# Loading the second pieces of six early groups through ScalarE's DMA queue instead of SyncE's

## Chip, cores, metric

One core of a Trainium2 chip. The metric is the device time of one execution in microseconds (us), as the median of several executions; smaller is better. A profile shows a span about 2 us shorter than the time (96.6 us against 98.38 us for the profiled execution of the kernel before).

Words used below: **PE** is TensorE, **PEld** its weight loads, **DVE** VectorE, **ACT** ScalarE, **SPq** and **ACTq** the sequencers of SyncE and ScalarE, which issue transfers. A transfer "has landed" when the last of its 16 DMA engines has raised its completion semaphore.

## The reference

```python
rows, cols = 1024, 8192                       # x: float32
mean = np.mean(x, axis=-1, keepdims=True)
std = np.std(x, axis=-1, keepdims=True)
z = (x - mean) / (std + 1e-8)
return (np.mean(z ** 4, axis=-1) - 3).astype(np.float32)
```

The kurtosis of each row: 33.5 MB are read once and 4 KB written.

## The kernel before

The rows are cut into 18 groups, each laid over all 128 partitions. Groups 0 and 1 have 0.5 MB, group 2 has 1 MB, and groups 3 to 17 have 2 MB each, loaded in two to four pieces. I call the two pieces of group 3 "3a" and "3b", and so on.

```python
GROUPS = [                      # parts of a row, columns of each piece, columns of the 4th power on ACT
    (8, [1024], 0),             # group 0
    (8, [1024], 0),             # group 1
    (4, [2048], 0),             # group 2
    (2, [2048, 2048], 512),     # group 3: pieces 3a, 3b of 1 MB each
    # ... groups 4 to 12 are the same; 13 to 17 have three or four smaller pieces
]
SLOTS = 12                      # tiles of 2 MB for the data

def load(i):
    # ...
    c = 0
    for w in pieces:
        nc.sync.dma_start(out=xt[:, c:c + w], in_=src[:, c:c + w])
        c += w

def row_sums(i):                # groups 3 to 17: sums by 32 transposes on TensorE, first piece first
    # ...
    for c in range(0, w, P):
        nc.tensor.matmul(tps, lhsT=xt[:, c:c + P], rhs=ident,
                         start=c == 0, stop=c == w - P, is_transpose=True)
    nc.vector.tensor_reduce(out=red..., in_=tps..., op=AO.add, axis=AX)

def mean(i):
    nc.tensor.matmul(mps, lhsT=lhs, rhs=rhs, start=True, stop=True)
    nc.scalar.copy(nmu, mps)                       # "the copy": minus the mean

def square(i):
    nc.scalar.activation(out=xts[i], in_=xts[i], func=AF.Square, bias=nmus[i],
                         accum_out=sa[:, j:j + 1])

# fourth_act(i): 512 columns of the 4th power on ScalarE; fourth_dve(i): the rest on VectorE
# finish(b): for a batch of groups, two small matmul parts ("the reciprocal part" is the first),
#            a few small VectorE operations and a store

for i in range(NG):
    load(i)                     # every load stands ahead of all computing
waiting = []
for i in range(NG):
    row_sums(i)
    mean(i)
    square(i)
    # ... next step of a finish, fourth_dve(i - 1), fourth_act(i)
```

Each engine works through its own instructions in the order of the source. On TensorE, the mean of group 2 (it needs VectorE's sum of group 2) and the reciprocal part of the first batch (it needs the squares of groups 0 and 1) stand ahead of group 3's transposes.

## Time and profile before

| what | value | from |
|---|---|---|
| time, median of 2 | 98.88 us (98.24 to 99.53) | the runs |
| span | 96.6 us | the profile |
| busy: ACT, DVE, PE, PEld | 81, 75, 70, 64% | the page's part 1 |
| DMA engines full | slices 2 to 34 of 40, about 420 GB/s | the page's part 2 |
| last load landed | 84.58 us | semaphore events of the trace |
| square of group 3 begins | 18.86 us | timeline of ScalarE |
| square of group 17 begins | 86.80 us | timeline of ScalarE |

The slices give a first answer ("the DMA engines are full"), but they are an average over a start, a long middle and a tail. The timelines by engine tell what each stage waits for. A line of a timeline gives start, duration, engine, source line, operation, tiles; the bracket at its end is the idle time of the engine ahead of it and what ended that. The lines themselves are in the prediction below.

### The profile page before, as it was taken

Reading aid. Unit: us, or ns where it says so; the run is one execution under the profiler, and the core shown is the slowest. Engines: PE = TensorE matmul, PEld = TensorE weight load, DVE = VectorE, ACT = ScalarE, POOL = GpSimd, SP = SyncE. Lnnn points to the kernel's source line nnn. Section 1 sums busy time; section 2 is a strip of 40 time slices with the busy share of each in tenths; the row PEclk is TensorE's granted clock in tenths of the full one; section 3 lists DMA queues with packets and bytes.
Section 4 is the critical chain, followed back from the end, with each engine's and each line's share of the span. In section 5 each row is a group of like instructions: output and inputs, shape, how many; then the busy total and the mean of one; then the engine's idle time right before and its main releaser. Section 6 shows DMA issues by size and latency. Waiting matters only on the chain.

```text
span 96.6 us, 1451 instructions
## 1 busy us (share of the span) xinstructions
PE 67.5 (70%) x540; PEld 61.4 (64%) x540; DVE 72.2 (75%) x74; ACT 77.9 (81%) x86; POOL 4.7 (5%) x20
## 2 busy tenths in 40 slices
PE   0040699797959597979797979797978797950120
PEld 0040699696949496969686868696967696940010
DVE  0238600653969998989898989798989698999470
ACT  6055540299979889999999999899999899989960
POOL 6830000000000000000000000000000000000000
PEclk9999999999999999999999999999999999998555
DMA  1999999999999999999999999999999999200000
GB/s 47 398 395 410 420 427 427 434 431 424 414 410 424 434 417 417 417 431 427 400 431 417 431 404 420 395 427 407 423 409 421 407 419 395 113 1 0 0 0 0
DMA packets 5658, 33.64 MB, mean 348 GB/s; under 512 B 660, under 2 KB 660, under 8 KB 2964
## 3 DMA queue, kind: packets, MB, share of 16 engines
q1 hardware_dynamic: 5652, 33.56, 84.5%
q8 instruction: 4, 0.07, 0.3%
q14 instruction: 2, 0.02, 0.0%
HBM read 33.55 MB, written 0.00 MB: 347 GB/s over the span
## 4 chain that ended last, share of the span: by engine, by line
DMA 72%; PE 13%; ACT 7%; SPq 3%; DVE 2%; issue 1%; ACTq 0%
DMA xt<-in_x_dram 72%; PE tps L132 10%; ACT xt L158 4%; SPq L120 3%; ACT xt L165 3%; DVE red L135 1%; PE mps L151 1%; PE p L191 1%; PE p L192 0%; DVE kr L194 0%; PE p L182 0%; DVE kr L195 0%; ACTq L252 0%; ACTq L158 0%; ACT nmu L153 0%
## 5 line engine op out<-in xcount | busy, mean ns | idle before, releaser
L171 DVE CUSTOM_DVE_ANT_0 xt<-xt 128x3584 f32<-128x3584 f32 (+3 forms) x18 | 60.6, 3365 | 1.9 <-ACT nmu L153 1.1
L158 ACT ACTIVATE xt<-xt,nmu 128x4096 f32<-128x4096 f32 (+2 forms) x18 | 60.1, 3342 | 0.8
L132 PE MATMUL tps<-ident,xt 128*128 128x128 f32 x480 | 59.6, 283 | 1.0 <-DMA xt<-in_x_dram 1.0
L132 PEld LDWEIGHTS tps<-ident,xt 128*128 128x128 f32 x480 | 55.5, 148 | 3.1 <-DMA xt<-in_x_dram 2.6
L135 DVE TENSOR_REDUCE red<-tps 128x128 f32<-128x256 f32 x15 | 6.3, 423 | 11.7 <-PE tps L132 11.4
L153 ACT COPY nmu<-mps 128x1 f32<-128x1 f32 x18 | 2.7, 151 | 13.2 <-PE mps L151 13.2
L151 PEld LDWEIGHTS mps<-negcol,red 128*128 128x128 f32 x30 | 4.5, 188 | 13.1 <-ACT xt L158 6.5
L151 PE MATMUL mps<-negcol,red 128*128 128x1 f32 x30 | 5.4, 248 | 9.9 <-DVE red L135 7.0
L165 ACT ACTIVATE xt<-xt 128x512 f32<-128x512 f32 (+1 forms) x15 | 11.4, 759 | 0.5
L151 PE MATMUL mps<-part,blk 128*128 128x1 f32 x6 | 1.7, 353 | 9.0 <-DVE part L143 9.0
L151 PEld LDWEIGHTS mps<-part,blk 128*128 128x128 f32 x6 | 1.5, 312 | 9.2 <-POOL blk L78 5.2
L143 DVE CUSTOM_DVE_ANT_0 junk<-xt 128x512 bf16<-128x512 f32 (+1 forms) x3 | 2.7, 916 | 4.1 <-DMA xt<-in_x_dram 4.1
L182 PE MATMUL p<-blk,sa 128*2 128x16 f32 (+3 forms) x8 | 1.2, 232 | 4.2 <-ACT xt L158 4.2
L158 ACT ACTIVATION_READ_ACCUMULATOR xt<-xt,nmu 128x1 f32 x18 | 3.3, 185 | 0.0
L184 DVE RECIPROCAL rec<-p 2x16 f32<-2x16 f32 (+3 forms) x4 | 1.7, 418 | 2.1 <-PE p L182 2.1
L182 PEld LDWEIGHTS p<-blk,sa 128*2 128x2 f32 (+3 forms) x8 | 0.4, 84 | 4.3 <-issue 4.3
L165 ACT ACTIVATION_READ_ACCUMULATOR xt<-xt 128x1 f32 x15 | 2.8, 187 | 0.0
L191 PE MATMUL p<-blk,sa 128*2 128x16 f32 (+3 forms) x8 | 1.2, 233 | 2.2 <-ACT xt L165 2.2
L191 PEld LDWEIGHTS p<-blk,sa 128*2 128x2 f32 (+3 forms) x8 | 0.4, 84 | 2.5 <-ACT xt L165 2.5
L68 ACT ACT_TABLE_LOAD x1 | 1.3, 1283 | 0.8 <-PEq L241 0.8
L194 DVE TENSOR_TENSOR kr<-p,rec 2x16 f32<-2x16 f32 (+3 forms) x4 | 0.8, 189 | 1.4 <-PE p L192 1.4
L81 POOL TENSOR_SCALAR_AFFINE_SELECT blk<-blk 128x128 f32<-128x128 f32 x3 | 1.7, 564 | 0.2
(18 smaller groups left out, 8.7 us busy)
## 6 DMA issues: line engine op xcount, KB each, us to landing
xt<-in_x_dram SPq DMA_DIRECT2D x21, 1024.0 KB, 20.1
xt<-in_x_dram SPq DMA_DIRECT2D x9, 768.0 KB, 14.1
xt<-in_x_dram SPq DMA_DIRECT2D x6, 512.0 KB, 15.0
xt<-in_x_dram SPq DMA_DIRECT2D x1, 640.0 KB, 13.5
xt<-in_x_dram SPq DMA_DIRECT2D x1, 384.0 KB, 12.6
xt<-in_x_dram SPq DMA_DIRECT2D x1, 256.0 KB, 11.3
out_dram<-kr SPq DMA_DIRECT2D x2, 0.1 KB
out_dram<-kr SPq DMA_DIRECT2D x1, 3.0 KB
```

The source lines that it names most:

```text
L81: nc.gpsimd.affine_select(out=v, in_=v, pattern=[[k, r], [0, k]], base=k - 1, channel_multiplier=-1, compare_op=AO.is_ge, fill=0.0)
L120: nc.sync.dma_start(out=xt[:, c:c + w], in_=src[:, c:c + w])
L132: nc.tensor.matmul(tps, lhsT=xt[:, c:c + P], rhs=ident, start=c == 0, stop=c == w - P, is_transpose=True)
L135: nc.vector.tensor_reduce(out=red.rearrange("p (r k) -> p r k", k=k), in_=tps.rearrange("p (r k) -> p r k", k=k).unsqueeze(2).to_broadcast ...
L143: nc.vector.tensor_tensor_reduce(out=junk[:, :w // 2], in0=xt[:, :w // 2], in1=xt[:, w // 2:], scale=1.0, scalar=0.0, op0=AO.add, op1=AO.a ...
L151: nc.tensor.matmul(mps, lhsT=lhs, rhs=rhs, start=True, stop=True)
L153: nc.scalar.copy(nmu, mps)
L158: nc.scalar.activation(out=xts[i], in_=xts[i], func=AF.Square, bias=nmus[i], accum_out=sa[:, j:j + 1])
L165: nc.scalar.activation(out=xts[i][:, :c], in_=xts[i][:, :c], func=AF.Square, accum_out=sa[:, n + j:n + j + 1])
L171: nc.vector.tensor_tensor_reduce(out=t, in0=t, in1=t, scale=1.0, scalar=0.0, op0=AO.mult, op1=AO.add, accum_out=sd[:, j:j + 1])
L184: nc.vector.reciprocal(rec, p2)
L191: nc.tensor.matmul(p4, lhsT=sa[:, n:2 * n], rhs=sel, start=True, stop=False)
```

## The change

The intent is to let two queues issue loads, so that more transfers are handed over at the start and SyncE has less to issue. Six of the 39 loads move; nothing else changes.

```diff
+TWO_QUEUES = range(3, 9)
...
-        for w in pieces:
-            nc.sync.dma_start(out=xt[:, c:c + w], in_=src[:, c:c + w])
+        for j, w in enumerate(pieces):
+            queue = nc.scalar if i in TWO_QUEUES and j == 1 else nc.sync
+            queue.dma_start(out=xt[:, c:c + w], in_=src[:, c:c + w])
             c += w
```

Pieces 3b, 4b, 5b, 6b, 7b and 8b are now issued by ScalarE, ahead of all its computing.

## The prediction

> **What bounds the kernel now.** I read the page's 40 slices first, then the chain that ended last, then the waits of SyncE's DMA queue, then the timelines of ScalarE and TensorE by stage.
>
> ```profile
> DMA  1999999999999999999999999999999999200000
> DMA 72%; PE 13%; ACT 7%; SPq 3%; DVE 2%; issue 1%; ACTq 0%
> SPq L120 <- DMA xt<-in_x_dram: 57.0, 29, 3.0
> ```
>
> The reader sees that the 16 DMA engines are full from the second slice to the 34th, at some 420 GB/s, and that most of the chain is transfers. The third line (the waits of SyncE's queue: total us, times, longest) says that SyncE never lags: 29 times it waited for an earlier transfer to land. Its issue records show why. The program gives its transfers eight completion semaphores in turn, and the ninth waits for the semaphore of the first, and so on, so eight are in flight. One issue takes 0.33 to 0.59 us, and one 1 MB piece leaves every 2.48 us (issues at 8.69, 11.15, 13.63, 16.11), which is the rate of the data. So SyncE's issue time costs nothing now.
>
> The bound by transfers is thin, though: ScalarE has almost no slack behind them.
>
> ```profile
> 5.80 0.16 ACT L153 COPY nmu<-mps 128x1 f32<-128x1 f32 x1 [3.51 <-PE mps L151]
> ...
> 11.03 2.00 ACT L158 ACTIVATE xt<-xt,nmu 128x2048 f32<-128x2048 f32 x1
> 12.93 0.19 ACT L158 ACTIVATION_READ_ACCUMULATOR xt<-xt,nmu 128x1 f32 x1
> 18.62 0.16 ACT L153 COPY nmu<-mps 128x1 f32<-128x1 f32 x1 [5.50 <-PE mps L151]
> 18.86 3.72 ACT L158 ACTIVATE xt<-xt,nmu 128x4096 f32<-128x4096 f32 x1
> ...
> 39.02 3.73 ACT L158 ACTIVATE xt<-xt,nmu 128x4096 f32<-128x4096 f32 x1
> 42.65 0.18 ACT L158 ACTIVATION_READ_ACCUMULATOR xt<-xt,nmu 128x1 f32 x1
> 42.87 0.63 ACT L165 ACTIVATE xt<-xt 128x512 f32<-128x512 f32 x1
> 43.40 0.19 ACT L165 ACTIVATION_READ_ACCUMULATOR xt<-xt 128x1 f32 x1
> 43.49 0.14 ACT L153 COPY nmu<-mps 128x1 f32<-128x1 f32 x1
> 43.67 3.72 ACT L158 ACTIVATE xt<-xt,nmu 128x4096 f32<-128x4096 f32 x1
> ```
>
> (Timeline of ScalarE: start us, us, what, and in brackets the idle time before it.) Group 0 begins at 5.80, group 2 is squared at 11.03, group 3 at 18.86, and from 34.38 to 57.62 one square follows the other every 4.65 us with no wait in brackets: there ScalarE sets the pace. The square of the last group, 17, begins at 86.80. Between groups 3 and 17 lie 14 steps, 67.94 us. Of these the three from group 3 to 6 take 15.52 us (the waits there are for VectorE and TensorE, not for data), and the other eleven would take 11 x 4.65 = 51.15 us at ScalarE's pace. Together 66.67, so data costs only 67.94 - 66.67 = 1.27 us there. **If group 3 is squared later by D, the end moves by about D - 1.27 us.**
>
> **What the Trainium skill says.** "DMA: Bandwidth & Descriptors", section "Issuing engines are not separate DMA queues", says that transfers started by SyncE or ScalarE run on the same 16 DMA engines, and that a second issuer saves only the sequencer's issue time. The trace before agrees that there is nothing else to gain: the engines are full and the issuer waits 57.0 us. Section "Queues, rings and completion order" says that a DMA engine takes turns between its queues packet by packet; the trace before has all loads on one queue and cannot show it. "Advanced Engine Details and Errata", section "Sequencer and Instruction Queues", has one sequencer read an engine's instructions in order, so an issue on ScalarE that waits holds back the squares behind it; before, ScalarE issues nothing. "TensorE: Matmul & The Clock Gate", Part 1, has a cold array at half clock; here 27 of group 3's 32 transposes have weight loads 0.21 us apart, later ones 0.11.
>
> **The change part by part.** Groups 3 to 8 have pieces a and b of 1 MB each; the six b pieces move to ScalarE's queue. Bytes, sizes and slots stay.
>
> *Removed from SyncE:* six issues of 0.33 to 0.59 us, about 2.5 us, all of it in front of a full pipe. Worth 0.
>
> *Added to ScalarE:* six issues, some 2.5 us in all. The source loads every group before it computes any, so all six stand ahead of group 0's copy. I assume that the eight semaphores still go round in the source's order, over both queues. Numbering from 0, the b pieces are transfers 4, 6, 8, 10, 12, 14. The first two are free; 8 waits for transfer 0 (group 0), 10 for transfer 2 (group 2), 12 for transfer 4 (3b), 14 for transfer 6 (4b). **ScalarE cannot begin group 0 before group 2 and 4b have landed and three more issues are done.** That is the cost I expect to dominate.
>
> *Moved data.* With two queues the pieces land in another order. From the issue times before, the landing time by MB transferred is: 0.5 at 4.2 us, 1 at 5.4, 2 at 8.7, 3 at 11.1, 4 at 13.6, and 2.48 per MB from there. Group 2 (1 MB, after groups 0 and 1 of 0.5 MB each) and 4b (after 3b) need 4 MB in all, whatever the order, so 13.6 us is the earliest. Packets are one row: 4 KB in groups 0 and 1, 8 KB after. If turns go by packet and both queues start together, ScalarE's moves 2 MB while SyncE's moves groups 0 and 1 (3 MB in all), then group 2 shares evenly with 5b, and lands at 5 MB, 16.1 us. If ScalarE starts late by half a MB, behind its table load (0.79 to 2.07), both land at 4 MB. I take 4.6 MB, 15.1 us. Three issues of 0.4 make 16.3 us, against 5.80 when group 0 began: range 14.8 to 17.4.
>
> *From there to group 3.* TensorE is in order, and the reciprocal part of batch one (it needs the squares of groups 0 and 1) and the mean of group 2 stand ahead of group 3's transposes. Before, copy of group 0 to the first of those transposes took from 5.80 to 11.18; without the waits for data in it, 5.1 us. So transposes begin at 16.3 + 5.1 = 21.4. Piece 3a, now third on a queue with half the engines' time, lands at 5.5 to 7 MB, 17.3 to 21.0 us, just in time. From first transpose to square of group 3 before: 18.86 - 11.18 = 7.68 us.
>
> ```profile
> 11.18 6.51 PE L132 MATMUL tps<-ident,xt 128*128 128x128 f32 x32 [0.28 <-DMA xt<-in_x_dram]
> 18.20 0.38 PE L151 MATMUL mps<-negcol,red 128*128 128x1 f32 x2 [0.52 <-DVE red L135]
> ```
>
> (Timeline of TensorE: 32 transposes in 6.51 us, against 3.71 for the next group.) I keep the cold 6.51, since TensorE would idle even longer ahead of them. Square of group 3: 21.4 + 7.68 = 29.1 us, D = 29.1 - 18.86 = 10.2, less 1.27 makes 9.0 us.
>
> *The sum.* 0 - 0 + 9.0: 98.88 + 9.0 = 107.9, say 107.8 us. Transfers still end near 84 us: bytes and rate are the same, and the slots that loads of groups 12 to 17 wait for come free early enough even 10 us late (group 5's, free at 37.4 before, is wanted at 68.3).
>
> **Rivals.**
> *One: ScalarE isn't held.* The semaphores might be dealt out by queue. For it: nothing in the trace, which has one queue alone; against: eight semaphores were used strictly in turn. ScalarE would issue six times 0.4 us from about 1 us, done by 3.5, ahead of its first work at 5.80. But data order still bites: 3a on half the engines lands at 6 to 7 MB, 18.6 to 21.0 us instead of 11.1; plus 7.68 gives 26.3 to 28.7, D of 7.4 to 9.8, end at 105 to 107.4.
> *Two: no sharing by turns, pieces land in order of issue.* 3a would land near 11 to 13 us, and ScalarE still be held until 13.6 + 1.2 = 14.8: square of group 3 at 14.8 + 5.1 + 7.68 = 27.6, end at 106.4. With rival one true as well, nothing would change: 98.9.
> *Three: SyncE's queue is served ahead*, having six or seven pieces waiting against two. Then 4b lands only after up to 8 MB, 23.5 us, and the end moves to some 115.
> *Four: two queues feed the DMA engines better.* They are at 9 tenths or more in 32 slices, and the end would be held by ScalarE anyway. At most 1.27 us, unless ScalarE isn't delayed.
>
> **Range and chances.** My own spread of the hold (14.8 to 17.4) gives 106.4 to 109.0. A TensorE that is warm by then would take off up to 2.8; rival one takes off up to 3; unequal turns add a few. Eight in ten: 104.5 to 111.0. Slower by over 2% needs only 2 of the 9 us: 0.94. Same, 0.05; faster, 0.01, for which the profile gives no source.
>
> **What would show it.** Six issues on ScalarE ahead of its first copy, the last waiting for a load; the first copy near 16.3 instead of 5.80; group 3's transposes near 21.4 and its square near 29.1; squares after group 6 at 4.65 us each to the end, with no waits for data; the last square near 96 instead of 86.80; transfers still ending near 84, the chain with a smaller share of DMA and a larger of ScalarE. I am wrong if ScalarE's first copy comes near 6 us, if the pace later falls below 4.65, or if 3a lands as early as before.

## The result and the profile after

The changed kernel takes **105.22 us** (104.73 to 105.72, 2 runs) against 98.88 us; the ratio is 1.064, with a 95% interval of 1.046 to 1.083. A repeat with more runs gave 104.81 us and 1.063 (1.055 to 1.071).

The slices of the changed kernel (part 2 of its page):

```profile
DMA  2999999999999999999999999999999910000000
```

A slice is now 2.58 us long. The DMA engines are as full as before and done as early: the last load landed at 84.30 us, against 84.58. No transfer time was lost. The span grew by 6.4 us behind it.

The chain that ended last, first line, of the changed kernel:

```profile
ACT 15%; PE 1%; issue 0%; DVE 0%; ACTq 0%
```

Before, 72% of the chain was DMA. Now the part of it that the profile could follow (from 83.64 us on) is almost only ScalarE's squares. Its shares are of the whole span and sum to 16%, so this line tells what the end waits for, and nothing of the start.

The timeline of ScalarE shows the start of the changed kernel:

```profile
0.79 1.28 ACT L69 ACT_TABLE_LOAD   x1 [0.79 <-PEq L243]
0.97 1.34 ACTq L122 DMA_DIRECT2D xt<-in_x_dram  x3
2.09 0.20 ACT L69 ACTIVATE warm<-warm 128x1 f32<-128x1 f32 x1
9.55 2.82 ACTq L122 DMA_DIRECT2D xt<-in_x_dram  x3
12.41 0.16 ACT L155 COPY nmu<-mps 128x1 f32<-128x1 f32 x1 [10.12 <-DMA xt<-in_x_dram]
...
17.05 0.16 ACT L155 COPY nmu<-mps 128x1 f32<-128x1 f32 x1 [1.83 <-PE mps L153]
17.29 2.00 ACT L160 ACTIVATE xt<-xt,nmu 128x2048 f32<-128x2048 f32 x1
19.20 0.19 ACT L160 ACTIVATION_READ_ACCUMULATOR xt<-xt,nmu 128x1 f32 x1
26.17 0.16 ACT L155 COPY nmu<-mps 128x1 f32<-128x1 f32 x1 [6.79 <-PE mps L153]
26.41 3.72 ACT L160 ACTIVATE xt<-xt,nmu 128x4096 f32<-128x4096 f32 x1
```

Three issues pass at once, beside the table load. The other three wait until 9.55 and 12.04 us for earlier transfers, and ScalarE sits idle behind them: its first copy comes at 12.41 instead of 5.80, with the bracket "10.12 <-DMA". That is the hold that the prediction spoke of. But it is not the last wait. The copy of group 3 waits 6.79 us more, for TensorE.

The timeline of TensorE over the same stretch:

```profile
16.94 0.22 PE L184 MATMUL p<-blk,sa 128*2 128x16 f32 x2
19.53 5.70 PE L134 MATMUL tps<-ident,xt 128*128 128x128 f32 x32 [2.37 <-DMA xt<-in_x_dram]
25.75 0.38 PE L153 MATMUL mps<-negcol,red 128*128 128x1 f32 x2 [0.52 <-DVE red L137]
```

The reciprocal part, which the hold delays, is done at 16.94 + 0.22 = 17.16 us. Then TensorE waits 2.37 us longer, for data: **the first piece of group 3, still on SyncE's own queue, had not landed.** The semaphore events of the traces give these landing times in us:

| piece | queue after | before | after |
|---|---|---|---|
| group 0 | SyncE | 4.20 | 4.97 |
| 3b | ScalarE | 13.61 | 7.64 |
| group 1 | SyncE | 5.42 | 9.53 |
| 4b | ScalarE | 18.58 | 12.02 |
| group 2 | SyncE | 8.67 | 14.52 |
| 5b | ScalarE | 23.56 | 16.99 |
| **3a** | SyncE | **11.13** | **19.48** |
| 6b | ScalarE | 29.36 | 21.96 |
| 4a | SyncE | 16.10 | 24.45 |

From 9.53 us on, the two queues' pieces land strictly in turn, one each 2.5 us. Pieces that are needed later have taken half of the engines from pieces that are needed first.

After the start nothing new happens. Squares of groups 3 and 17 begin at 26.41 and 93.17 us, 66.76 us apart; before it was 67.94, of which 1.2 us were waits for data that are gone now.

### The profile page after: what moved, and what is told of

Read it like the earlier page. It is cut to its first block, busy times and chain, and to the rows that moved or that the text cites. A ratio compares the mean times of both kernels' runs of the same rounds, so it can differ in the third digit from the quotient of the medians.

```text
span 103.0 us, 1450 instructions
## 1 busy us (share of the span) xinstructions
PE 65.4 (64%) x540; PEld 60.7 (59%) x540; DVE 71.8 (70%) x74; ACT 77.6 (75%) x86; POOL 4.6 (4%) x20
## 5 line engine op out<-in xcount | busy, mean ns | idle before, releaser
L134 PE MATMUL tps<-ident,xt 128*128 128x128 f32 x480 | 57.5, 280 | 2.4 <-DMA xt<-in_x_dram 2.4
L134 PEld LDWEIGHTS tps<-ident,xt 128*128 128x128 f32 x480 | 54.8, 146 | 3.0 <-DMA xt<-in_x_dram 2.5
```

The lines of the kernel that those rows point to most:

```text
L134: nc.tensor.matmul(tps, lhsT=xt[:, c:c + P], rhs=ident, start=c == 0, stop=c == w - P, is_transpose=True)
```

## The experiments

Two theories. **A, the hold:** ScalarE's computing waits behind its own issues. **B, the order of landing:** two queues share the DMA engines by turns, so that 3a comes late, whoever issues. The prediction had it as second in importance.

### Three pieces on ScalarE, none of which waits

```diff
-TWO_QUEUES = range(3, 9)
+TWO_QUEUES = range(3, 6)
```

> Only the second pieces of groups 3, 4 and 5 go to ScalarE; all three have a free semaphore, so ScalarE waits for none and its first copy should come near 6.5 us. Theory A (the hold of ScalarE costs the time): time of before, 98.9 us. Theory B (piece 3a comes late because two queues share the DMA engines by turns): 3a lands when ScalarE's 3 MB and SyncE's first 3 MB are in, near 18.2 us, transposes of group 3 begin there, 1.2 us earlier than in the changed kernel: 104.0 us.

Measured: 103.64 us, ratio 1.052 (1.048 to 1.056). ScalarE's first copy came at 5.84 us, as in the kernel before, so there was no hold at all, and still five sixths of the loss are there. ScalarE's first copy and TensorE's timeline in this run:

```profile
5.84 0.16 ACT L155 COPY nmu<-mps 128x1 f32<-128x1 f32 x1 [3.56 <-PE mps L153]
```

```profile
16.26 0.22 PE L184 MATMUL p<-blk,sa 128*2 128x16 f32 x2
17.92 5.66 PE L134 MATMUL tps<-ident,xt 128*128 128x128 f32 x32 [1.44 <-DMA xt<-in_x_dram]
```

3a landed at 17.87 and the transposes began at 17.92. Even the reciprocal part is late (16.26), because group 2 landed at 14.26 instead of 8.67. Theory A alone has fallen. The last sixth fits the landing too: with six pieces 3a comes 1.6 us later than with three (19.48 against 17.87), and the span is 1.6 us longer (103.0 against 101.4).

### One piece, two pieces: the dose

```diff
-TWO_QUEUES = range(3, 9)
+TWO_QUEUES = range(3, 4)      # one piece; range(3, 5) in the run with two
```

> Only 3b goes to ScalarE. Theory A: 98.9 us. Theory B, as a dose: 3a lands after 4 MB, near 13.6 us instead of 11.1; group 3's transposes begin there, square of group 3 at 20.5 to 21.3, so the end is 0.4 to 1.2 us later than before: 99.3 to 100.1 us.

> The dose between: 3b and 4b on ScalarE, no hold. 3a lands after 5 MB, near 15.6 us, square of group 3 near 22.7, and each us of it beyond some 20 moves the end by one: 100.7 us. If the hold were the cause: 98.5.

Measured: 98.58 us for one piece, ratio 1.002 (0.999 to 1.004); 100.77 us for two, ratio 1.020 (1.010 to 1.031), which the 2% rule calls unclear. 3a landed at 13.13 and 16.00 us, and the transposes began at 13.17 and 16.05. One piece costs less than the least that I expected.

In the profiled executions 3a is 2.0, 4.9 and 6.7 us late with one, two and three pieces, the square of group 3 is 1.7, 4.1 and 5.9 us late, and the span is 0.6, 3.0 and 4.8 us longer. Past a slack of some 1.15 us, each us by which the square is late is paid in full. The medians show the same order with less precision (0.1, 2.2 and 5.2 us): the four runs with two pieces fell into two pairs (100.07 and 100.25, 101.28 and 101.34), the profiled one is of the slower pair, and nothing on record tells what differs between the pairs.

### The hold alone

All loads stay on SyncE. ScalarE first makes a square that needs 3a, into a tile that nobody reads.

```diff
     for i in range(NG):
         load(i)
+    held = const.tile([P, 1024], bf16, name="held")
+    nc.scalar.activation(out=held, in_=xts[3][:, :1024], func=AF.Square)
```

> All loads on SyncE as before, but ScalarE first squares 1024 columns of 3a into a scratch tile, so that its first copy comes near 12.4 us as in the changed kernel. If only the landing of 3a counts: 98.9 us. If the hold counts as well, in parallel: group 3's transposes begin near 17.2 us (4.75 after the copy), its square at 24.1 to 24.9, end 4.0 to 4.8 us later than before: 102.9 to 103.7 us.

Measured: 102.13 us, ratio 1.038 (1.032 to 1.044). ScalarE's and TensorE's timelines of this run, two lines each:

```profile
11.72 1.06 ACT L202 ACTIVATE held<-xt 128x1024 bf16<-128x1024 f32 x1 [9.44 <-DMA xt<-in_x_dram]
12.68 0.14 ACT L153 COPY nmu<-mps 128x1 f32<-128x1 f32 x1
```

```profile
17.19 0.22 PE L182 MATMUL p<-blk,sa 128*2 128x16 f32 x2
17.34 5.32 PE L132 MATMUL tps<-ident,xt 128*128 128x128 f32 x32
```

With the copy at 12.68, the transposes begin at 17.34 with no wait for data in the bracket. The start was about as expected (17.2). The time is 0.8 us under the range: some half of that is that the kernel before took 98.45 us in these rounds and not the 98.9 that I had counted from, the rest that the transposes took 5.32 us, not the 5.7 to 6.5 that I had carried over. So a hold of this size is worth some 3.7 us **where the data are there**. The mechanism of the prediction is real.

### Three pieces and the hold

The two causes together, without touching the order of landing of the first experiment: three pieces on ScalarE, and a square of 1024 columns of 4b ahead of the first copy.

```diff
-TWO_QUEUES = range(3, 9)
+TWO_QUEUES = range(3, 6)
...
+    held = const.tile([P, 1024], bf16, name="held")
+    nc.scalar.activation(out=held, in_=xts[4][:, 2048:3072], func=AF.Square)
```

> Three second pieces on ScalarE (103.6 us) and besides a hold of ScalarE's first copy to some 12.7 us by a square of 1024 columns of 4b into a scratch tile. If the hold and the late landing add up: 106 to 107.4 us. If they lie beside each other: the reciprocal part is done near 17.4 us, still ahead of 3a's landing near 17.9, so 103.6 us again.

Measured: 103.54 us, ratio 1.050 (1.043 to 1.058), against 103.64 us without the hold. ScalarE's first copy moved from 5.84 to 12.84 us, and the time stayed. TensorE's timeline shows why:

```profile
17.35 0.22 PE L184 MATMUL p<-blk,sa 128*2 128x16 f32 x2
18.12 5.99 PE L134 MATMUL tps<-ident,xt 128*128 128x128 f32 x32 [0.55 <-DMA xt<-in_x_dram]
```

The held path is done at 17.57 us, and 3a lands at 18.08. The two delays lie beside each other, and the later one counts.

### First pieces instead of second pieces

```diff
-            queue = nc.scalar if i in TWO_QUEUES and j == 1 else nc.sync
+            queue = nc.scalar if i in TWO_QUEUES and j == 0 else nc.sync
```

> The changed kernel with the first pieces of the six groups on ScalarE instead of the second: 3a lands near 7.6 us and 3b near 19.5. ScalarE is held as before (first copy near 12.4). If the hold alone set the end: 105.2 us as in the changed kernel. If 3a's landing sets it: TensorE does the first half of group 3's transposes from 17.2 us and the rest by 23 to 23.7, square at 24.1 to 24.9: 102.9 to 103.7 us.

Measured: 101.79 us, ratio 1.034 (1.030 to 1.039): 3.0 us better than the repeat of the changed kernel (104.81), with the same number of bytes on each queue. The hold was the same (first copy at 12.32). 3a landed at 7.57 and 3b at 19.39. TensorE's timeline:

```profile
16.84 0.22 PE L184 MATMUL p<-blk,sa 128*2 128x16 f32 x2
17.00 5.25 PE L134 MATMUL tps<-ident,xt 128*128 128x128 f32 x32
```

TensorE could spend the wait for 3b on the transposes of 3a, so 3a and 3b no longer bind; what ends last is the held path: 17.00 us, near the 17.34 of the run with the hold alone. But it ends last by little. VectorE's timeline shows the path, the 4th power of group 0 (after its held square) and behind it the sum of group 2:

```profile
13.83 1.22 DVE L173 CUSTOM_DVE_ANT_0 xt<-xt 128x1024 f32<-128x1024 f32 x1 [3.55 <-ACT nmu L155]
14.98 1.22 DVE L145 CUSTOM_DVE_ANT_0 junk<-xt 128x1024 bf16<-128x1024 f32 x1
```

The sum of group 2 begins at 14.98 us, and group 2 itself had landed only at 14.41 (at 9.22 in the run with the hold alone). Without the hold this path would be shorter by an estimated 0.6 us (14.98 - 14.41): with three pieces and no hold, group 2 landed at 14.26 and the reciprocal part was done at 16.48. So this run does not show a loss by the hold alone; most of the delay is the late landing of group 2, which the hold covers. The same holds for the changed kernel (15.08 and 14.52).

The result is 1.1 us under the expected range, in part because the 32 transposes took 5.25 us, in part because I had again counted from 98.9 us.

### Two queues in the order of need

Four transfers on ScalarE, one more than in the first experiment, chosen so that the turns follow the order of use: group 1, 3a, 4a and 5a on ScalarE; group 0, group 2, 3b and 4b on SyncE.

```diff
-TWO_QUEUES = range(3, 9)
+TWO_QUEUES = (1, 3, 4, 5)
...
-            queue = nc.scalar if i in TWO_QUEUES and j == 1 else nc.sync
+            queue = nc.scalar if i in TWO_QUEUES and j == 0 else nc.sync
```

> Four transfers on ScalarE, all with free semaphores, but chosen so that the two queues take turns in the order of need: group 1, 3a, 4a and 5a on ScalarE, the rest on SyncE. If a second queue is bad in itself: 1 to 5 us slower, as with two or three pieces. If only the order of landing counts: group 2 and 3a land together near 10.6 us, 3b near 15.6, transposes of group 3 from 12.7, square near 19.9, which is within the slack: 98.5 us, the time of before.

Measured: 98.14 us against 98.61 us for the kernel before on the same chip, ratio 0.9968 (0.9949 to 0.9988). It is some 0.3% better than the kernel before. TensorE's timeline:

```profile
12.03 0.22 PE L184 MATMUL p<-blk,sa 128*2 128x16 f32 x2
12.19 5.91 PE L134 MATMUL tps<-ident,xt 128*128 128x128 f32 x32
```

Group 2 and 3a landed at 10.04 and 10.78 us, 3b at 15.01, and nothing waited for data there. Square of group 3 began at 19.27 us, 0.4 later than before and within the slack; the last load landed at 84.20 us, 0.4 earlier than before. A second queue is not slow in itself. No run shows where the 0.3% comes from.

### The changed kernel again

> The changed kernel once more, beside the next three on one chip: 104.7 to 105.7 us; group 3's transposes begin when 3a lands (19.5 us) and its square near 26.4.

Measured: 104.81 us (4 runs), first copy at 12.19, 3a landed at 19.47, transposes from 19.51, square of group 3 at 26.51.

### All profiles in one table

"Ready" is the end of the reciprocal part on TensorE, the last thing ahead of group 3's transposes. Times are us of each run's profile.

| kernel | ready | 3a landed | transposes begin | square of group 3 | span | span less square | median time |
|---|---|---|---|---|---|---|---|
| before | 10.90 | 11.13 | 11.18 | 18.86 | 96.6 | 77.7 | 98.88 |
| four, in order of need | 12.25 | 10.78 | 12.19 | 19.27 | 96.3 | 77.0 | 98.14 |
| one piece | 12.86 | 13.13 | 13.17 | 20.58 | 97.2 | 76.6 | 98.58 |
| two pieces | 15.74 | 16.00 | 16.05 | 22.98 | 99.6 | 76.6 | 100.77 |
| first pieces | 17.06 | 7.57 | 17.00 | 23.42 | 100.0 | 76.6 | 101.79 |
| hold alone | 17.41 | 11.70 | 17.34 | 23.84 | 100.4 | 76.6 | 102.13 |
| three pieces | 16.48 | 17.87 | 17.92 | 24.75 | 101.4 | 76.7 | 103.64 |
| three and hold | 17.57 | 18.08 | 18.12 | 25.29 | 101.9 | 76.6 | 103.54 |
| changed kernel | 17.16 | 19.48 | 19.53 | 26.41 | 103.0 | 76.6 | 105.22 |
| changed kernel, again | 16.94 | 19.47 | 19.51 | 26.51 | 103.1 | 76.6 | 104.81 |

Two rules hold in every row. The transposes begin at the later of "ready" and "3a landed", to within 0.1 us (ends on TensorE are modelled, hence the small negative ones). And once the square of group 3 comes later than about 20 us, the span is that time plus 76.6 us.

## Why the prediction was right or wrong

- **SyncE's issue time was worth nothing, and transfers end at the same time:** right. The last load landed at 84.30 us (84 predicted), and the DMA engines gained 0.3 us at most.
- **The delay of group 3's square moves the end, less a slack of 1.27 us:** right. Before, the span was 77.7 us past that square, in the changed kernel 76.6, so the slack measured 1.15. From group 3 to group 17 it took 66.76 us; 66.67 was predicted.
- **"ScalarE cannot begin group 0 before group 2 and 4b have landed":** wrong in its first half. This is the step that failed. It took the eight semaphores to be dealt out in the source's order. In the trace ScalarE's fourth issue waits for group 1 (landed 9.53), and not for group 2 (14.52): within each pair of pieces, ScalarE's was numbered ahead of SyncE's. Three MB had to land instead of four, and the first copy came at 12.41 us, neither the 16.3 predicted nor within the spread of 14.8 to 17.4. That a waiting issue holds back the work behind it at all was the prediction's inference from the page that it cites, which doesn't state it; the runs show it (the copy at 12.41 us behind the last issue at 12.04, and at 5.84 where no issue waits).
- **"That is the cost I expect to dominate":** wrong for this kernel. From the copy to "ready" took 17.16 - 12.41 = 4.75 us (5.1 predicted), and then 2.37 us passed in a wait for 3a. The prediction had 3a at 17.3 to 21.0 and "just in time"; it landed at 19.48 and set the start. A hold of this size costs 3.7 us where data are early and nothing where they are late.
- **First transpose to square in 7.68 us, with a cold TensorE:** oversized. It took 26.41 - 19.53 = 6.88 us, since the 32 transposes took 5.70 instead of 6.51. The reason given for keeping 6.51, a longer idle time ahead of them, didn't hold: TensorE idled 2.37 us there instead of 0.28, and the slow stretch was shorter (4.1 us instead of 5.8 by the spacing of the weight loads).
- **The sum:** transposes from 19.53 instead of 21.4 (-1.9), a shorter cold stretch (-0.8) and a slack smaller by 0.1 (+0.1) make -2.6 us, which is the distance from 107.8 to 105.2. That the number still came near is partly luck: the path that was to set the start was done 4.2 us early (17.16 instead of 21.4), and the landing of 3a, which the prediction had as "just in time", happened to fall only 1.9 us short of the start that was predicted. The order of landing was the prediction's rival one, which reckoned that it alone, without a hold, would end at 105 to 107.4; the 105.2 measured lies at the low end of that.
- **Turns by packets of one row, so that 4 KB rows get half the share of 8 KB rows:** nearly right. The DMA packets in the changed kernel's trace, counted by queue, show it: from 5.5 to 8.5 us, with both queues at work, 113 packets of 4 KB began on SyncE's queue and 98 of 8 KB on ScalarE's, so the bytes went 1 to 1.7. The late start of ScalarE's queue, which the prediction allowed for with half a MB, was there too: its first packet began at 3.23 us, SyncE's at 1.83, and SyncE had then moved about 0.35 MB. By 9.53 us SyncE's queue had moved 1.08 MB and ScalarE's 1.73.
- **Slips in its sums:** the DMA row has 33 slices at 9 tenths, not 32, and rival three adds up to 116 us, not 115. Neither matters to the forecast.
- **Rivals two, three and four:** not seen. Pieces landed by turns and not in the order of issue; SyncE's queue had more waiting and wasn't preferred.

What stays open: why the program numbers ScalarE's piece ahead of SyncE's within a pair was only observed.

## What to carry to other kernels

Here the DMA engines were full, and a second issuing queue added no bandwidth (the last load landed at 84.30 us instead of 84.58); it changed which bytes came first. Put pieces on two queues so that taking turns gives the order of use, and put nothing that is needed late on the queue that is otherwise empty. Before moving issues to a computing engine, list which completion semaphores they will wait for, and look at both paths that meet at the next consumer: the later one is the cost, so taking away the other one shows nothing.

## What the Trainium skill lacked or had wrong

- "DMA: Bandwidth & Descriptors", section "Issuing engines are not separate DMA queues", says that several issuers' transfers interleave on the same engines and only save issue time. It lacks what the interleaving can cost, because it reorders what lands: 3a moved from 11.13 to 19.48 us and the kernel lost 6.3%, with the engines equally full.
- The same page, section "Queues, rings and completion order", has turns packet by packet between queues. For rows of 8 KB on both queues the traces agree (landings alternate each 2.5 us). For 4 KB rows against 8 KB rows the page gives no figure; here 113 packets of 4 KB began beside 98 of 8 KB (5.5 to 8.5 us).
- "TensorE: Matmul & The Clock Gate", Part 1, has a warm-up of about 3.4 us whose end varies by half a us; it also says that the number of cold matmuls changes from run to run. By the spacing of the weight loads, group 3's transposes stayed at half rate for 3.2 to 5.8 us in the ten traces (5.8 before, 4.1 in the changed kernel, 3.2 with first pieces).
- No page says that a program's completion semaphores can tie two queues together: with eight in turn over both, ScalarE's fourth issue waited until 9.55 us for a transfer of SyncE's (group 1, landed at 9.53).
